# Two modulation vectors computed during the linear attention instead of during the latent attention

## The chip, the cores and the metric

The kernel runs on one core of a Trainium2 chip. The metric is the device time of one execution in microseconds (us); runs of one kernel are summed up by their median. The core has a matrix engine (TensorE, PE in the profile, with its weight loads shown as PEld), three engines for elementwise work (VectorE = DVE, ScalarE = ACT, GpSimd = POOL) and a queue engine (SyncE = SP) that issues most of the transfers between main memory and on-chip memory. Each engine takes its own instructions strictly in the order in which the program gives them, and waits on semaphores for the others.

## The reference, cut to what matters

One layer of a streaming encoder for 1024 prompt tokens and 64 sample tokens. Six vectors of length 1024 per stream (the modulation) are computed from a conditioning vector; the layer uses them at different places.

```python
mod = silu(c) @ w_ada + b_ada                      # w_ada: 1024 x 6144
shift1, scale1, gate1, shift2, scale2, gate2 = split(mod, 6)
h = rms_norm(x, g_norm1) * (1 + scale1) + shift1
proj = h @ w_in
c_q, c_kv, k_rope, gq, gk, gv, g_lr, g_r = split(proj)
a_out = latent_attention(c_q, c_kv, k_rope, ...)   # "latent attention", softmax over keys
b_out = gated_linear_attention(gq, gk, gv, g_lr) * silu(g_r)   # recurrence over chunks of tokens
x = x + gate1 * (concat(a_out, b_out) @ w_out)
h2 = rms_norm(x, g_norm2) * (1 + scale2) + shift2
x = x + gate2 * (square(relu(h2 @ w_up)) @ w_down)
```

The vectors are numbered 0 (shift1), 1 (scale1), 2 (gate1), 3 (shift2), 4 (scale2), 5 (gate2). Vectors 2 to 5 are not needed before the output projection, which comes after both attentions.

## The kernel before, in words

The program writes its work as Python generators ("streams"). `interleave` steps through several of them with a clock of its own: a stream yields how long its last piece keeps PE busy (`pe`), how long it then has to wait (`wait`), and a condition for going on. Of the streams that are ready the first in the list goes next. This gives an order of the program; a scheduler behind it then places each instruction on its engine's queue where its own estimate sees it ready, within the buffers that the program has. The result is one fixed order for each engine.

The stages, with the times of the profile of before:

- 0 to 94 us: the first norm, vectors 1 and 0, and the projection's first two groups of weight columns (A0, A1: queries and keys of the linear attention).
- 94 to about 290 us: the linear attention. The stream `gla` works through nine tiles of tokens (eight of 128, one of 64). For each tile it makes masked scores at seven levels (from halves of 64 tokens down to single ones): DVE and POOL prepare the level's operands `KL` and `QL` (L666 to L675), PE multiplies them (L729), DVE copies the masked result into `ST` (L732). The state `SB` goes on from tile to tile (L746, L755), and L769 and L773 form the tile's output, which ACT and DVE normalise (`og`, L778 and L781) and PE transposes later (L787). Beside it the stream `main` computes the rows of groups B0 and B1 (values, and the gate's low rank input `gl`), in eight steps of three matmuls for each tile of tokens (lines 93 to 95, 128x264), and from the gate rows of a chunk of three tiles the decays `bcum`: transposes L580, a matmul L585, ACT, and the scans L594 on DVE. From about 190 us `main` goes on with the columns of groups C0 and C1, and `latents` with D1.
- to about 388 us: query latents and the keys of the cached frames.
- 388 to about 606 us: the latent attention: keys, queries and three `worker` streams that take score matmuls (L971), softmax, transposes (L1008) and value matmuls (L998). The stream `mods` runs beside them and computes vectors 2, 4, 3, 5 in this order; it needs one of the four PSUM banks named `mm`, which the workers share.
- then the output projection, the second norm and the MLP, to the end.

One modulation vector is `mod_vec(m, ...)`: eight steps over the 1024 rows of `w_ada`. Each step has one 512 KB piece (`raw`, 128x1024) loaded by SP (L155) and four matmuls (L166) whose stationary side is 32 columns wide, one for each 32-column strip of the array, all into one bank. With `ahead=3` the first three pieces are loaded at once, and piece k+3 when step k has been written. After step eight ACT copies the bank (`lat`, L174), PE transposes it in two pieces (L178) and DVE adds the bias (`modT`); vector 4 takes two more small DVE operations (`G12`).

The pieces lie in the pool `rawp`, which has three buffers under one name. The same three buffers hold the raw pieces of `w_in`, which `loader` brings for the next group and which ACT and DVE then split into two halves `wh` and `wl` (L207, L213). `loader` starts group number j once group j-2 has been used up ("end B0" for C0).

```python
        for k in range(KT):
            yield 0, wait, None
            wait = min(wait, after)
            ...
            for j in range(4):
                mm = PE.matmul(acc[32 * j:32 * j + 32, 0:256], lhsT=scT[:, k, :], rhs=was[k][:, 256 * j:256 * (j + 1)],
                               start=(k == 0), stop=(k == KT - 1), tile_position=(0, 32 * j))
            if k + ahead < KT and ahead:
                load(k + ahead)
            yield 500, 0, None
```

## Time and profile before

| | |
|---|---|
| median of 3 runs | 1396.76 us (1396.51 to 1401.75) |
| the profiled execution's own time | 1395.58 us |
| its span, first to last instruction | 1393.8 us, mean granted TensorE clock 0.995 |
| PE busy over the span | 1338.4 us |
| DVE, ACT, POOL busy | 899.3, 654.4, 134.5 us |
| transferred | 188.15 MB, 135 GB/s on average |

The profiled execution's time is 1.8 us longer than its span: what lies before the first and after the last instruction. The profile's views used below are: the page (busy time of each engine, the chain of work that ended last); busy time by stretches, whose columns are the stretch, its length, the busy us and number of records of PE, PEld, DVE, ACT and POOL, then the granted clock (1.00 is full speed), the share of time in which the transfer engines moved data, and GB/s; the timeline of one engine, whose columns are start, length, engine, line, operation and shapes, with a number of records merged in a row and, in brackets, how long the engine stood idle before it and what ended that; and the list of waits. A 4-byte matmul as in L166 or L729 leaves two records.

### The profile page before, as it was taken

Reading aid. Unit: us, or ns where it says so; the run is one execution under the profiler, and the core shown is the slowest. Engines: PE = TensorE matmul, PEld = TensorE weight load, DVE = VectorE, ACT = ScalarE, POOL = GpSimd, SP = SyncE. Lnnn points to the kernel's source line nnn. Section 1 sums busy time; section 2 is a strip of 40 time slices with the busy share of each in tenths; the row PEclk is TensorE's granted clock in tenths of the full one; section 3 lists DMA queues with packets and bytes.
Section 4 is the critical chain, followed back from the end, with each engine's and each line's share of the span. In section 5 each row is a group of like instructions: output and inputs, shape, how many; then the busy total and the mean of one; then the engine's idle time right before and its main releaser. Section 6 shows DMA issues by size and latency. Waiting matters only on the chain.

```text
span 1393.8 us, 26311 instructions
## 1 busy us (share of the span) xinstructions
PE 1338.4 (96%) x10014; PEld 1257.6 (90%) x10014; DVE 899.3 (65%) x2034; ACT 654.4 (47%) x1623; POOL 134.5 (10%) x248
## 2 busy tenths in 40 slices
PE   6999899988999999999998999999999999999998
PEld 5898788887876778899998999999999999999998
DVE  5688777337565766656798756566545866874554
ACT  5465454235345566653475544544444343343342
POOL 0026445111011210000000000000000000000000
PEclk9999999999999999999999999999999999999999
DMA  9320021394253442164225444344348764543440
GB/s 345 121 73 9 16 73 45 114 249 124 86 158 119 152 133 61 52 200 137 78 81 178 159 150 150 128 156 143 102 172 286 281 219 154 184 127 95 125 129 33
DMA packets 165592, 188.15 MB, mean 135 GB/s; under 512 B 16814, under 2 KB 116442, under 8 KB 165466
## 3 DMA queue, kind: packets, MB, share of 16 engines
q1 hardware_dynamic: 158010, 180.90, 40.5%
q10 hardware_dynamic: 7456, 5.57, 1.2%
q8 instruction: 79, 1.29, 0.4%
q14 instruction: 47, 0.39, 0.1%
HBM read 132.97 MB, written 53.46 MB: 134 GB/s over the span
## 4 chain that ended last, share of the span: by engine, by line
PE 80%; DVE 10%; DMA 4%; ACT 3%; POOL 2%; issue 2%; SPq 0%; ACTq 0%; DVEq 0%; POOLq 0%
PE mm L93 14%; PE mm L95 14%; PE mm L94 14%; PE g L93 5%; PE g L95 5%; PE g L94 5%; PE mm L971 3%; PE tp L93 3%; PE tp L95 3%; PE tp L94 3%; PE g L998 3%; PE mm L166 2%; DMA raw<-in_w_in 1%; PE tp L1008 1%; DVE ST L732 1%
## 5 line engine op out<-in xcount | busy, mean ns | idle before, releaser
L101 ACT CAST opers<-quad 128x512 fp32r<-128x512 f32 x112 | 69.5, 620 | 185.0 <-PE mm L95 146.2
L102 DVE TENSOR_TENSOR opers<-quad,opers 128x512 fp32r<-128x512 f32 x112 | 77.3, 690 | 114.0 <-ACT opers L101 114.0
L95 PE MATMUL mm<-opers 128*128 128x272 f32 x448 | 128.9, 288 | 0.0
L93 PE MATMUL mm<-opers 128*128 128x272 f32 x448 | 128.5, 287 | 0.3 <-DVE e L1785 0.3
L94 PE MATMUL mm<-opers 128*128 128x272 f32 x448 | 128.3, 286 | 0.0
L93 PE MATMUL mm<-ah,wh 128*128 128x272 f32 x424 | 122.2, 289 | 4.2 <-ACT wh L101 2.2
L94 PE MATMUL mm<-al,wh 128*128 128x272 f32 x424 | 121.5, 287 | 0.0
L95 PE MATMUL mm<-ah,wl 128*128 128x272 f32 x424 | 121.4, 288 | 0.0
L93 PE MATMUL mm<-hh,wh 128*128 128x384 f32 (+2 forms) x264 | 90.6, 347 | 1.7 <-ACT hh L101 1.7
L95 PE MATMUL mm<-hh,wl 128*128 128x384 f32 (+2 forms) x264 | 87.4, 332 | 0.0
L94 PE MATMUL mm<-hl,wh 128*128 128x384 f32 (+2 forms) x264 | 87.3, 331 | 0.0
L93 PEld LDWEIGHTS mm<-opers 128*128 128x128 f32 x448 | 84.6, 189 | 0.5 <-issue 0.5
L93 PEld LDWEIGHTS mm<-ah,wh 128*128 128x128 f32 x424 | 79.8, 188 | 5.3 <-ACT wh L101 2.6
L95 PEld LDWEIGHTS mm<-opers 128*128 128x128 f32 x448 | 84.3, 188 | 0.0
L94 PEld LDWEIGHTS mm<-opers 128*128 128x128 f32 x448 | 84.0, 188 | 0.0
L94 PEld LDWEIGHTS mm<-al,wh 128*128 128x128 f32 x424 | 79.7, 188 | 0.0
L95 PEld LDWEIGHTS mm<-ah,wl 128*128 128x128 f32 x424 | 79.5, 188 | 0.0
L102 DVE TENSOR_TENSOR opers<-ru,opers 128x544 fp32r<-128x544 f32 x108 | 77.6, 720 | 2.1 <-ACT opers L101 2.0
L101 ACT CAST opers<-ru 128x544 fp32r<-128x544 f32 x108 | 69.4, 643 | 13.1 <-PE mm L95 11.7
L101 ACT CAST wh<-ru 128x512 fp32r<-128x512 f32 x67 | 41.3, 618 | 67.4 <-PE g L94 24.5
L102 DVE TENSOR_TENSOR wl<-ru,wh 128x512 fp32r<-128x512 f32 x67 | 46.0, 690 | 36.4 <-ACT wh L101 36.1
L93 PE MATMUL mm<-wh,hh 128*128 128x264 f32 (+3 forms) x216 | 66.2, 308 | 0.2 <-ACT wh L213 0.2
(409 smaller groups left out, 4338.8 us busy)
## 6 DMA issues: line engine op xcount, KB each, us to landing
ru<-u_d SPq DMA_DIRECT2D x108, 272.0 KB, 2.8
raw<-in_w_ada SPq DMA_DIRECT2D x40, 512.0 KB, 4.0
ru<-in_w_up SPq DMA_DIRECT2D x32, 512.0 KB, 4.1
quad<-in_w_down SPq DMA_DIRECT2D x16, 1024.0 KB, 7.0
u_d<-st SPq DMA_DIRECT2D x60, 272.0 KB, 2.1
u_d<-sc SPq DMA_DIRECT2D x45, 272.0 KB, 2.1
raw<-in_w_in SPq DMA_DIRECT2D x22, 256.0 KB, 4.0
x<-in_xo_T SPq DMA_DIRECT2D x8, 544.0 KB, 5.1
```

What stands on the lines that cost most here:

```text
L93: PE.matmul(out, lhsT=ah, rhs=bh, start=first, stop=False, skip_group_check=more)
L94: PE.matmul(out, lhsT=ah, rhs=bl, start=False, stop=False, skip_group_check=more)
L95: PE.matmul(out, lhsT=al, rhs=bh, start=False, stop=last, skip_group_check=more)
L101: ACT.copy(hi, src)
L102: eng.tensor_tensor(out=lo, in0=src, in1=f32(hi), op=ALU.subtract)
L166: mm = PE.matmul(acc[32 * j:32 * j + 32, 0:256], lhsT=scT[:, k, :], rhs=was[k][:, 256 * j:256 * (j + 1)], start=(k == 0), stop=(k == KT - ...
L732: DVE.copy_predicated(ST[:n, :, :n].rearrange("p c (b r h) -> p c b r h", r=2, h=hf)[:, :, :, 1], masks[:n, mlv, :n // 2].rearrange("p (o ...
L971: PE.matmul(sp[:n, :w], lhsT=x[:, hd, :n], rhs=y[:, hd, :w], start=(j == 0), stop=(j == 4))
L998: PE.matmul(op[:n, 0:P], lhsT=pt[:kw, k, :n], rhs=kvs[kt // 4].v[:kw, kt % 4, hd], start=(kt == 0), stop=(kt == nkt - 1))
L1008: PE.transpose(tp[:kw, k, :n], pr[k0 // 4][:n, P * k:P * k + kw], ident[:n, :n])
```

## The change

Vectors 2 and 4 leave the stream `mods` of the latent attention. A new stream `mods_first` computes them in the linear attention's stage, from the moment at which group B1 is split. It stands in the list behind `gla` and ahead of `main`, so that in `interleave` a step of it goes before rows of B0 and B1 that are ready at the same time. It uses the same three `rawp` buffers, the pool `dp` for the copy of the bank, and one `mm` bank; the step's wait is given as `after=5000`, but `mod_vec` starts at 3500 and takes the smaller of the two, so a step waits 3500 there too. Group C0's loads now wait for "mods 2" as well, since they need the same three buffers.

```diff
@@ loader
             if j >= 2:
-                yield from load_group(key, w_in_cols(a, b), 8, b - a, after=has("end " + GROUPS[j - 2][0]))
+                yield from load_group(key, w_in_cols(a, b), 8, b - a,
+                                      after=has("end " + GROUPS[j - 2][0], *(["mods 2"] if key == "C0" else [])))
@@ linear attention's stage
+        def mods_first():
+
+            yield 0, 2000, has("B1")
+            for m in (2, 4):
+                yield from mod_vec(m, rawp, "raw", dp, mm_bank, 3, after=5000)
+            done.add("mods 2")
+
         lats = Stream(latents())
-        interleave([weights, gla(), main(), gates(), lats], rest=(weights, lats))
+        interleave([weights, gla(), mods_first(), main(), gates(), lats], rest=(weights, lats))
@@ latent attention's stage
     def mods():
-        for m in (2, 4, 3, 5):
+        for m in (3, 5):
```

What this makes of the engines' orders is shown at three places. (Lines from 249 on stand one to eight lower in the changed program: L729 is L730 there, L746 is L747, L773 is L774.)

The first is PE near the end of the linear attention's first tile, in the profile of before from 111.71 to 118.88 us: the tile's state matmul (`kt_`), its last four levels (`QL`, `KL`), the next tile's diagonal (`pr`) and the tile's output (`ST`). Before:

```order
L746 MATMUL g<-gv,kt__1175 128x256 x2
L729 MATMUL g<-QL_904,KL_901 128x128 x2
L729 MATMUL g<-QL_905,KL_902 128x128 x2
L729 MATMUL g<-QL_906,KL_903 128x128 x2
L729 MATMUL g<-QL_904,KL_901 128x128 x2
L705 MATMUL g<-indi,pr 128x2 x2
L773 MATMUL mm<-gv,ST 128x128 x4
```

Now, from the row ahead of the state matmul on:

```order
L166 MATMUL mm<-raw,scT 32x256 x4
L747 MATMUL g<-gv,kt__1185 128x256 x2
L730 MATMUL g<-QL_904,KL_901 128x128 x2
L166 MATMUL mm<-raw,scT 32x256 x3
L730 MATMUL g<-QL_905,KL_902 128x128 x2
L730 MATMUL g<-QL_906,KL_903 128x128 x2
L166 MATMUL mm<-raw,scT 32x256
L730 MATMUL g<-QL_904,KL_901 128x128 x2
L166 MATMUL mm<-raw,scT 32x256 x2
L706 MATMUL g<-indi,pr 128x2 x2
L166 MATMUL mm<-raw,scT 32x256 x5
L774 MATMUL mm<-gv,ST 128x128 x4
```

Between the matmuls of this tile now stand the vector's steps four to eight (their first five matmuls stand a little ahead of these rows, before the tile's third level).

The second is PE where the gates of the second chunk of tiles are made, in the profile of before at 150.98 us: the last `gl` transpose and the gate matmul (`glrT`, `wg`), on whose result the next three tiles' decays rest. Before:

```order
L729 MATMUL g<-QL_905,KL_902 128x128 x2
L769 MATMUL mm<-SB_907,qe 128x256
L580 MATMUL tp<-ident,gl 16x128
L93 MATMUL mm<-wh,hh 128x264
L94 MATMUL mm<-wl,hh 128x264
L95 MATMUL mm<-wh,hl 128x264
L93 MATMUL mm<-wh,hh 128x264
L585 MATMUL g<-glrT_892,wg 128x384 x2
```

Now:

```order
L730 MATMUL g<-QL_906,KL_903 128x128 x2
L166 MATMUL mm<-raw,scT 32x256
L581 MATMUL tp<-ident,gl 16x128
L166 MATMUL mm<-raw,scT 32x256 x3
L770 MATMUL mm<-SB_907,qe 128x256
L586 MATMUL g<-glrT_892,wg 128x384 x2
L774 MATMUL mm<-gv,ST 128x128 x2
L770 MATMUL mm<-SB_907,qe 128x256
L774 MATMUL mm<-gv,ST 128x128 x2
```

The second vector's sixth step stands ahead of the gate matmul, cut in two by the transpose; 14 of the 16 steps stand ahead of it in all. From the fourth tile's state matmul on, PE's order in this stage is that of before again, but for a few exchanges.

The third is SP's queue in the same stage, from the loads of B0 and B1 on. `SB` is the state, `mix_d<-mog` a tile's finished output. Before:

```order
L207 DMA raw<-in_w_in 128x2x264 x8
L207 DMA raw<-in_w_in 128x2x256
L541 DMA wg<-in_b_gate_up 1x256
L207 DMA raw<-in_w_in 128x2x256 x2
L557 DMA SB_909<-in_state_gla 64x128 x4
L791 DMA mix_d<-mog 128x4x128 x4
L207 DMA raw<-in_w_in 128x2x256 x4
```

Now:

```order
L207 DMA raw<-in_w_in 128x2x264 x8
L155 DMA raw<-in_w_ada 128x1024
L542 DMA wg<-in_b_gate_up 1x256
L155 DMA raw<-in_w_ada 128x1024 x2
L558 DMA SB_909<-in_state_gla 64x128 x4
L155 DMA raw<-in_w_ada 128x1024 x9
L792 DMA mix_d<-mog 128x4x128
L155 DMA raw<-in_w_ada 128x1024 x3
L792 DMA mix_d<-mog 128x4x128
L155 DMA raw<-in_w_ada 128x1024
L207 DMA raw<-in_w_in 128x2x256 x3
L792 DMA mix_d<-mog 128x4x128 x2
```

The three early pieces of C0 (128x2x256) have given their places to the vectors' first pieces, and come behind the vectors' sixteenth; the first tile's output stands behind nine loads that wait for PE.

## The prediction

> **What bounds the kernel now.** I read the page first, then the chain of waits, then busy time by stretches of the two stages that the change touches.
>
> ```profile
> PE 1338.4 (96%) x10014; PEld 1257.6 (90%) x10014; DVE 899.3 (65%) x2034; ACT 654.4 (47%) x1623; POOL 134.5 (10%) x248
> PE 80%; DVE 10%; DMA 4%; ACT 3%; POOL 2%; issue 2%; SPq 0%; ACTq 0%; DVEq 0%; POOLq 0%
> ```
>
> PE is the bound of the whole, at 96% busy and 80% of the chain. But the 4% that it lacks lie in few places, so I look at the stretches (stretch, length, then busy us of PE, PEld, DVE, ACT, POOL, granted clock, transfer share, GB/s):
>
> ```profile
> 94.00:124.00 30.00, 25.15 (x158) 22.18 (x157) 22.19 (x71) 16.27 (x57) 17.07 (x34) 0.89 0.07 20
> 124.00:152.00 28.00, 26.71 (x200) 24.51 (x199) 20.55 (x64) 8.80 (x33) 11.77 (x22) 1.00 0.07 20
> 152.00:176.00 24.00, 19.31 (x124) 16.47 (x123) 19.83 (x61) 15.01 (x53) 14.68 (x25) 0.94 0.04 12
> ...
> 196.00:290.00 94.00, 91.14 (x583) 82.56 (x582) 54.83 (x153) 39.59 (x128) 27.36 (x54) 1.00 0.36 108
> ...
> 462.00:535.00 73.00, 71.73 (x532) 57.52 (x532) 48.96 (x142) 44.93 (x145) 10.35 (x14) 1.00 0.44 140
> 535.00:606.00 71.00, 69.65 (x497) 64.64 (x496) 46.77 (x136) 46.37 (x117) 2.66 (x4) 1.00 0.26 76
> ```
>
> The vectors leave a stage in which PE idles 1.27 of 73 and 1.35 of 71 us (462 to 606). They enter one that has idle time: 4.85 us in 94 to 124, 1.29 in 124 to 152, 4.69 in 152 to 176. The transfers are nearly at rest there (share 0.04 to 0.07), so the 8 MB of `w_ada` find room. The question is how much of the idle time lies where the new matmuls are put, and what stands behind them. PE's timeline shows whose waits they are:
>
> ```profile
> 103.86 0.71 PE L729 MATMUL g<-QL,KL 128*128 128x128 f32 x4 [1.39 <-POOL QL L675]
> 110.71 0.68 PE L729 MATMUL g<-QL,KL 128*128 128x128 f32 x4 [1.18 <-DVE sq L591]
> 118.88 2.08 PE L773 MATMUL mm<-gv,ST 128*128 128x128 f32 x8 [0.55 <-DVE dg L707]
> 141.92 0.27 PE L580 MATMUL tp<-ident,gl 128*16 128x128 f32 x1 [1.07 <-DVE gl L578]
> 150.98 1.55 PE L585 MATMUL g<-glrT,wg 33*128 33x384 f32 x4
> 158.90 0.70 PE L769 MATMUL mm<-SB,qe 128*128 128x256 f32 x2 [0.73 <-POOL qe L713]
> 160.01 0.68 PE L729 MATMUL g<-QL,KL 128*128 128x128 f32 x4 [0.41 <-DVE QL L675]
> ```
>
> Around 104 to 119 PE waits for the recurrence's elementwise work, and again from 158. Between, from 124 to 152, it is nearly full: the rows of the second chunk of three tiles have to be made before the gate matmul at 150.98, and DVE and POOL are waiting for that. Whatever is put ahead of the gate matmul in that piece delays it, and everything after it, one for one.
>
> There is a second loss in the stage, the granted clock:
>
> ```profile
> 108.00:110.00 2.00, 1.53 (x7) 0.93 (x6) 0.67 (x3) 1.94 (x6) 0.91 (x2) 1.00 0.00 0
> 110.00:111.00 1.00, 0.29 (x2) 0.32 (x3) 0.83 (x3) 1.00 (x4) 0.00 (x0) 1.00 0.00 0
> 112.00:113.00 1.00, 1.00 (x3) 0.76 (x3) 1.00 (x5) 0.65 (x2) 0.54 (x3) 0.50 0.00 0
> 121.00:122.00 1.00, 1.00 (x6) 1.00 (x6) 0.24 (x1) 1.00 (x8) 0.00 (x0) 0.50 0.00 0
> ```
>
> After a few sparse us (1.53 of 2 and 0.29 of 1 busy) the clock stands at 0.50, and again around 121. Over the 30 us the mean of 0.89 makes 3.3 us of lost clock; the output matmul at 118.88 takes 2.08 us in one of these holes.
>
> **The price of a vector's matmul on PE.** The change moves instructions that the trace shows elsewhere:
>
> ```profile
> 61.15 0.34 PE L94 MATMUL mm<-hl,wh 128*128 128x384 f32 x1
> 61.33 0.34 PE L95 MATMUL mm<-hh,wl 128*128 128x384 f32 x1
> 61.59 0.64 PE L166 MATMUL mm<-raw,scT 128*32 128x256 f32 x8
> 62.16 0.44 PE L93 MATMUL mm<-hh,wh 128*128 128x384 f32 x1
> 62.45 0.34 PE L94 MATMUL mm<-hl,wh 128*128 128x384 f32 x1
> ...
> 43.84 0.62 PE L166 MATMUL mm<-raw,scT 128*32 128x256 f32 x2
> 44.39 0.44 PE L94 MATMUL mm<-hl,wh 128*128 128x384 f32 x1
> ...
> 95.01 0.28 PE L95 MATMUL mm<-wh,hl 128*128 128x264 f32 x1
> 95.13 0.28 PE L93 MATMUL mm<-wh,hh 128*128 128x264 f32 x1
> ...
> 391.25 1.05 PE L166 MATMUL mm<-raw,scT 128*32 128x256 f32 x10
> 392.23 0.83 PE L1207 MATMUL g<-ones,sq 128*128 128x1 f32 x6
> ...
> 466.82 1.50 PE L166 MATMUL mm<-raw,scT 128*32 128x256 f32 x24
> ```
>
> Neighbours follow each other every 0.18 us (61.15 to 61.33). Four vector matmuls in a row (x8 records) run side by side and take 0.57 (61.59 to 62.16). But the step into them is 0.26 and the step out 0.29, where 0.18 each is usual: 0.2 us more. So a run of four costs 0.77. A single one takes 0.55 (43.84 to 44.39), so 0.75 with the same two steps: the price is by run, not by matmul. Five in a row take 0.98 (391.25 to 392.23), twelve 1.5. The Trainium skill (TensorEngine Tiling (Array Packing), Key Properties) says that a change of tiling mode drains the array; these rows agree, with 0.2 us for the two changes. It speaks against this change, which cuts the vectors into more runs: without the 0.2 they would cost 3 us more where they go than where they were, and with it, as counted below, 4.
>
> **What leaves the latent attention.** Up to about 462 us the order there is the old one, with vectors 3 and 5 in the places of 2 and 4. What goes is the second pair of places:
>
> ```profile
> 462.00:535.00 73.00, 10.42 (x128) 2.85 (x128) 1.00 0.44 140
> ...
> L178 PE MATMUL tp<-ident,lat x8: 270/273/293, 425.0 to 533.4; 128*128 128x128 f32 x8
> L174 ACT COPY lat<-mm x4: 372/374/395, 418.0 to 531.9; 128x256 f32<-128x256 f32 x4
> ...
> PE tp L893 <- DVE kn L886: 0.8, 1, 0.8
> ```
>
> The first row is L166 alone: 10.42 us busy for 128 records. By starts it is 9.5: thirteen runs of three or four at 0.57, one of one at 0.55, the run of twelve at 1.5. Fifteen runs at 0.2 add 3.0. The transposes are two pieces of two records for each vector, some 0.45 a vector as starts follow, 0.9 for two. That is 13.4 us off PE. All lie in a stage that is 98% PE; the work that is left has DVE at 49 and ACT at 45 of 73 us, and the `mm` bank that the vectors held until the last copy at 531.9 us is free for the workers. Some gaps that the vectors filled will open: the last row (a wait of PE: total, times, longest) shows one of 0.8 that such a run shortened. I give 1.0 back. If the cover is thinner (each of the fifteen runs was filling a gap of 0.2) it is 3 back. Gain: 12.4, with ends 10.4 and 13.4.
>
> **What enters the linear attention.** Counting runs in the new order: the first vector is cut into eleven (9.1 us: 6.9 by its own starts, among them two of five at 0.98, and 2.2 for the steps), the second into nine (7.4: 5.6 and 1.8). With 0.9 for transposes, 17.4 us come in where 13.4 go. By piece:
>
> 94 to 124: the first vector, 9.1. Its first and third steps stand ahead of gate matmuls, each cut in two, and delay the decays by 1.5 each. The second fills the 1.39 at 103.86; the fourth to eighth, 5.4 us in seven runs, meet the waits from 110 to 119 (1.18, 0.55 and the smaller ones between). Waits in the stretch: 4.85. And PE is then no longer sparse at 108 to 111, so I expect the clock to stay up: 3.3 back at most, since part of the slow clock ran under waits I take 2.0. Sum 9.1 - 4.4 - 2.0 = 2.7. Ends: 0.9 (all waits, all clock) and 7.5 (a third of the waits, no clock).
>
> The Trainium skill (TensorE: Matmul & The Clock Gate, Part 1) has the half clock set in after an idle window of about 3.4 us. Here the longest single wait ahead of it was 1.39 us, so the trace does not agree: a sparse window was enough. By the page's rule the fill could not be what restores the clock, and the sum would be 2.0 worse.
>
> 124 to 152: six steps of the second vector (eight runs, four whole and four cut: 6.1), the last of them on both sides of the `gl` transpose right ahead of the gate matmul, and one vector's transposes, 0.45. Four row matmuls (0.12 each, 95.01 to 95.13) have moved behind it: 0.5 off. The one long wait, 1.07 for `gl`, stays where it is, since the transpose still follows the row directly. Sum 6.1. Ends: 5.0 (the wait filled) and 6.6 (the row matmuls were no loss before).
>
> 152 to 176: steps seven and eight in one run, 1.3, stand just ahead of the wait of 0.73 and the next of 0.41 and fit in; the other transposes meet waits too. 0.
>
> ACT gets two copies (0.37 each, L174), DVE four small operations, both in the recurrence's idle; they stay inside the ends above.
>
> After 176 the order is the old one, and from 196 PE is 97% busy (91.14 of 94), so what PE has lost by then it does not win back: 2.7 + 6.1 + 0 = 8.8 us later.
>
> **Transfers and queues.** Nothing of this waits long by the rows:
>
> ```profile
> raw<-in_w_ada SPq DMA_DIRECT2D x40, 512.0 KB, 4.0
> ...
> 86.44 4.47 SPq L207 DMA_DIRECT2D raw<-in_w_in  x3
> ...
> 191.24 1.56 ACT wh L213 x3
> ```
>
> The first piece is issued about where C0's first was (the last of the three from 86.44 to 90.9) and lands at about 95, when PE comes to it. Later pieces have three buffers and 4.0 us; the tight ones are the seventh and eighth of the first vector, whose buffers, as I estimate from the timeline's starts and the new order, come free at about 113 and 114 and whose matmuls stand at about 117 and 118. C0's pieces are now loaded only after step 16, at about 170, and ACT took the first at 191.24. On SP the first tile's output waits behind nine loads; its buffer is wanted again one tile (some 16 us) later. All this costs 0, and 8 in the rival below.
>
> **Sum.** -12.4 + 8.8 = -3.6 us. The profiled execution (1395.58 us, span 1393.8 and 1.8 around it) becomes 1392.0. It lies 1.2 under the median of the three runs, 1396.76, so for the median I say 1393.2.
>
> **Rivals.**
>
> A, the forecast: 0.50; its own range 1390 to 1398 (12.4 against 0.9 + 5.0 and against 7.5 + 6.1).
>
> B, the waits take nearly all: the chain of the recurrence, not PE, sets the end of the stage. DVE is busy 19.83 of 24 us in 152 to 176, with 4.69 of PE idle there. If DVE starts those tiles better supplied, 3 of PE's 8.8 come back, and the 1.3 of clock that I left out as well: 4.5 later, -7.9 in all, 1389, and 1388 with the upper end of the gain. For it: the waits are real and the order was rearranged around them. Against it: the gate matmul is late for certain, and DVE with it. 0.24.
>
> C, nothing is absorbed: the runs stand a little beside the waits, the clock holes move rather than go, and gaps open in the latent attention: 7.5 + 6.6 against 10.4 is 3.7 later, 1400; with one end only, 1398 to 1399. Then the change is one that only moves PE's work. 0.15.
>
> D, slower: the ring of three buffers. If PE reaches the first vector's seventh and eighth steps before their pieces (4.0 us after their buffers come free), it stands in line, with the levels behind it, and DVE and POOL idle: up to 4.0 each, 8.0 on top of 8.8 is 16.8 against 12.4, 4.4 slower, 1401; with C's gaps up to 1405. It decides from a landing later than 117 us on. Against it: 0.07 transfer share, hence no contention. 0.11.
>
> **How the numbers follow.** Likeliest is A, 1393.2. For 8 in 10 I reach down over B to 1386.5 and up to 1400.5, over C and part of D. About 0.5% (7 us) is what a measurement of this kernel tells from no change: faster by more means under 1389.8, which is most of B and a tenth of A, 0.26; slower by more means over 1403.7, the far ends of C and D, 0.07; between them 0.67.
>
> **What would show it.** The first vector's runs between levels, PE idle in 94 to 124 down from 4.85 to about 1, and the clock near 1.00 there; the second chunk's gate matmul at about 159 to 160 rather than 150.98; the first columns of C0 about 9 us later; from there an unchanged distance to the latent attention; the last vector's transposes (L178) at about 470 instead of 533, and the output projection starting some 4 us earlier than before. I am wrong if the gate matmul moves by under 4 us (B), if a wait of PE for `raw` of over 1 us shows (D), or if the latent attention shortens by under 10 us.

## The result, and the profile after

The changed kernel takes 1401.10 us in the median of 19 executions (1398.89 to 1404.35), the kernel before 1398.39 beside it. The ratio is 1.0018, 95% interval 1.0011 to 1.0025: 2.5 us slower (1.5 to 3.5). That is within the 0.5% that I had called no change, but on the other side of it, and 0.6 us above the range that I gave. The forecast was 3.6 faster. One of the 19 executions of before took 3300.27 us, far outside all the others, and the ratio leaves it out.

The profiled execution takes 1401.34 us (span 1399.5, mean granted clock 0.994), 5.8 more than that of before (1395.58), twice what the medians differ by. So a pair of profiles has to be read with care here; why is shown below.

The page of the changed kernel says as little of it as that of before did: PE 96% busy, 80% of the chain.

```profile
PE 1344.2 (96%) x10014; PEld 1261.4 (90%) x10014; DVE 900.4 (64%) x2034; ACT 654.5 (47%) x1623; POOL 133.1 (10%) x248
PE 80%; DVE 9%; ACT 4%; DMA 3%; POOL 2%; issue 2%; SPq 0%; ACTq 0%; DVEq 0%; POOLq 0%
```

The same stretches as before in the linear attention, of the changed kernel (columns as in the prediction):

```profile
94.00:124.00 30.00, 28.02 (x205) 20.14 (x205) 20.56 (x67) 14.01 (x49) 14.70 (x28) 1.00 0.50 158
124.00:152.00 28.00, 26.78 (x214) 23.01 (x213) 19.15 (x62) 11.20 (x43) 12.83 (x26) 1.00 0.36 114
152.00:176.00 24.00, 22.32 (x167) 17.50 (x167) 17.19 (x55) 12.07 (x41) 9.49 (x18) 1.00 0.23 70
```

In 94 to 124 PE's idle time fell from 4.85 to 1.98 us and the clock went from 0.89 to 1.00. Still the gate matmul of the second chunk is late, and that of the third by as much (timeline of PE, after):

```profile
158.48 0.91 PE L586 MATMUL g<-glrT,wg 33*128 33x384 f32 x2
...
212.04 0.53 PE L586 MATMUL g<-glrT,wg 33*128 33x320 f32 x1
```

Of before the two stood at 150.98 and at

```profile
204.79 0.53 PE L585 MATMUL g<-glrT,wg 33*128 33x320 f32 x1
```

Lateness against before, by the same instruction in both traces:

| instruction | before, us | after, later by |
|---|---|---|
| gate matmul, second chunk | 150.98 | 7.5 |
| gate matmul, third chunk | 204.79 | 7.25 |
| last state matmul (L746) | 260.1 | 7.26 |
| first key transposes (L893) | 323.62 | 8.93 |
| first query transposes of the latent attention (L945) | 404.67 | 8.65 |
| its last output transposes (L1112) | 607.34 | 4.28 |
| last operation of the MLP (L1785) | 1390.23 | 5.67 |

The linear attention costs 7 to 9 us, as predicted. The latent attention gives back 4.4 where 12.4 were predicted. The 1.4 after it come with three stretches of half clock of 3.4 us each (from 727.0, 744.1 and 754.3 us), in code that the change doesn't touch; the profile of before has none there.

Where the gain went shows in the stretch from the old 462.0 to the last output transposes, of before and then of after:

```profile
462.00:607.30 145.30, 142.68 (x1039) 123.46 (x1039) 95.73 (x277) 91.44 (x263) 13.01 (x18) 1.00 0.36 110
```

```profile
470.60:611.60 141.00, 135.07 (x910) 122.59 (x910) 95.82 (x274) 91.27 (x261) 13.34 (x18) 0.99 0.21 61
```

PE is busy 7.6 us less, idle 3.3 more (5.93 against 2.62), and its clock has a hole. The biggest new wait and the hole stand together (timeline of PE, after):

```profile
475.06 0.28 PE L979 MATMUL mm<-kr,qrl 128*128 128x256 f32 x1
477.50 0.33 PE L1016 MATMUL tp<-ident,prob 128*128 128x128 f32 x1 [2.16 <-ACT prob L990]
...
480.69 0.52 PE L94 MATMUL g<-wl,cqh 128*128 128x384 f32 x1
481.01 0.46 PE L95 MATMUL g<-wh,cql 128*128 128x384 f32 x1
481.31 0.34 PE L93 MATMUL g<-wh,cqh 128*128 128x384 f32 x1
481.49 0.34 PE L94 MATMUL g<-wl,cqh 128*128 128x384 f32 x1
```

PE stands 2.16 us until ACT has the probabilities, and then takes 0.32 a matmul (480.69 to 481.01) where 0.18 is usual (481.31 to 481.49): half clock from 477.9 to 481.3, 1.6 us lost over eleven matmuls. In the kernel before the run of twelve vector matmuls (466.82, 1.5 us) stood in this place.

### The profile page after: what moved, and what is told of

Its sections match the earlier page's. It is cut to its first block, busy times and chain, and to the rows that moved or that the text cites. A ratio compares the mean times of both kernels' runs of the same rounds, so it can differ in the third digit from the quotient of the medians.

```text
span 1399.5 us, 26302 instructions
## 1 busy us (share of the span) xinstructions
PE 1344.2 (96%) x10014; PEld 1261.4 (90%) x10014; DVE 900.4 (64%) x2034; ACT 654.5 (47%) x1623; POOL 133.1 (10%) x248
## 4 chain that ended last, share of the span: by engine, by line
PE 80%; DVE 9%; ACT 4%; DMA 3%; POOL 2%; issue 2%; SPq 0%; ACTq 0%; DVEq 0%; POOLq 0%
PE mm L93 15%; PE mm L95 14%; PE mm L94 14%; PE g L93 6%; PE g L95 6%; PE g L94 6%; PE tp L93 3%; PE tp L95 3%; PE tp L94 3%; PE mm L979 2%; PE g L1006 2%; PE mm L166 2%; DMA raw<-in_w_in 1%; PE g L730 1%; PE tp L1016 1%
## 5 line engine op out<-in xcount | busy, mean ns | idle before, releaser
L95 PE MATMUL mm<-opers 128*128 128x272 f32 x448 | 128.9, 288 | 0.0
L94 PE MATMUL mm<-opers 128*128 128x272 f32 x448 | 128.3, 286 | 0.0
L94 PE MATMUL mm<-al,wh 128*128 128x272 f32 x424 | 121.8, 288 | 0.0
L95 PE MATMUL mm<-ah,wl 128*128 128x272 f32 x424 | 121.7, 289 | 0.0
L93 PE MATMUL mm<-hh,wh 128*128 128x384 f32 (+2 forms) x264 | 90.6, 347 | 1.4 <-ACT hh L101 1.4
L95 PE MATMUL mm<-hh,wl 128*128 128x384 f32 (+2 forms) x264 | 87.4, 332 | 0.0
L94 PE MATMUL mm<-hl,wh 128*128 128x384 f32 (+2 forms) x264 | 87.3, 331 | 0.0
L95 PEld LDWEIGHTS mm<-opers 128*128 128x128 f32 x448 | 84.3, 188 | 0.0
L94 PEld LDWEIGHTS mm<-opers 128*128 128x128 f32 x448 | 84.0, 188 | 0.0
L94 PEld LDWEIGHTS mm<-al,wh 128*128 128x128 f32 x424 | 80.0, 189 | 0.0
L95 PEld LDWEIGHTS mm<-ah,wl 128*128 128x128 f32 x424 | 79.9, 189 | 0.0
```

The lines of the kernel that those rows point to most:

```text
L93: PE.matmul(out, lhsT=ah, rhs=bh, start=first, stop=False, skip_group_check=more)
L94: PE.matmul(out, lhsT=ah, rhs=bl, start=False, stop=False, skip_group_check=more)
L95: PE.matmul(out, lhsT=al, rhs=bh, start=False, stop=last, skip_group_check=more)
```

## The experiments

Theories at the outset. **T1**: in the latent attention the vectors' runs filled waits for the softmax, so that taking them out opens the waits; in the linear attention the cost is the steps ahead of the gate matmul. **R1**: the runs were priced too high. **R2**: the new order, not the missing work, costs. **R3**: the linear attention's cost is no matter of the place ahead of the gates, or comes from something else. T2, T3, C1 and C2 came up on the way; the expectations say what they are, and the numbers of the experiments follow their names there.

One thing has to be known to read the numbers. A kernel's executions differ by up to 10 us, and most of that goes with the mean granted clock, which is listed for each. For the kernel before: 1399.8 us in the mean at 0.991 (17 executions), 1398.2 at 0.993 (22), 1396.8 at 0.995 (24). Within the changed kernel and those of the experiments together the slope is 1.0 us for 0.001 of clock (correlation 0.85 over 208 executions); for the kernel before alone it is 0.8 (0.80 over 150). So I split each difference from before into a part of the clock (1.0 us for each 0.001 that the mean clock is lower) and the rest, which is work and waits. The split is my own reckoning, good to some 0.5 us, and to 1 us where the clock's part is large. The first column is the ratio of the runs with its interval, turned into us:

| run | against before, us (95%) | of the clock | rest |
|---|---|---|---|
| the change | +2.5 (1.5 to 3.5) | -2.2 | +4.9 |
| E1 latent attention's part alone | -5.3 (-7.1 to -3.5) | +0.7 | -6.0 |
| E2 linear attention's part alone | +7.7 (5.7 to 9.6) | -2.9 | +10.1 |
| E7 as E1, old order | -4.1 (-6.2 to -2.0) | +0.8 | -4.3 |
| E8 empty steps in the linear attention | +0.3 (-1.3 to 1.8) | +0.2 | 0.0 |
| E9 the change, old order | +3.8 (2.1 to 5.5) | -1.3 | +4.8 |
| E3 the change, later places | +5.3 (3.8 to 7.0) | +1.1 | +4.2 |
| E12 as E1, second places kept | -1.0 (-2.5 to 0.6) | +4.3 | -5.3 |
| E10 the change, second places kept | +6.2 (3.9 to 8.2) | +0.6 | +6.0 |
| F1 E12 with matmuls of no use, misplaced | +1.3 (-0.7 to 3.2) | +4.2 | -3.4 |
| F4 E12 with such in the wait | -1.3 (-2.9 to 0.4) | +3.0 | -4.8 |
| F2 before with such | +1.7 (0.0 to 3.5) | -1.2 | +3.3 |
| F3 the change with such | +3.8 (2.2 to 5.3) | -1.0 | +5.0 |
| F5 the change, one transpose moved | +3.2 (1.4 to 5.0) | -1.4 | +4.8 |
| F6 E1, one transpose moved | -4.1 (-5.7 to -2.2) | +0.8 | -5.4 |
| E5 second vector later | +2.7 (1.3 to 4.1) | -1.7 | +4.4 |
| E4 one vector only | -1.4 (-3.1 to 0.1) | -3.4 | +1.7 |
| E11 as E4, three later places | +0.6 (-0.8 to 2.1) | -1.2 | +2.1 |
| G1 as E4, behind the rows | -4.6 (-6.2 to -3.1) | -2.8 | -1.5 |

(The two parts are of the difference of the means, so they don't always add up to the first column. For the change, the mean and the clock of before are those of the 150 executions beside the later runs.)

### E1 and E2: the two halves

E1 leaves vectors 2 and 4 out; E2 computes them twice.

```diff
-        for m in (2, 4, 3, 5):          # E1, from before
+        for m in (3, 5):
```
```diff
-        for m in (3, 5):                # E2, from the change
+        for m in (2, 4, 3, 5):
```

> The kernel before with vectors 3 and 5 alone in the latent attention; vectors 2 and 4 are left out altogether (ones stand in their place). So only what the change takes out of the latent attention is seen, none of what it puts into the linear attention. Price of the prediction: 12.4 us shorter than before. T1 (the vectors' runs were filler there: PE has less to do, but then waits for the softmax and loses some clock): 4 to 6 us shorter, with new PE waits on probabilities in the stretch where vectors 3 and 5 no longer follow 2 and 4. R1 (the runs were simply priced too high, no new waits): 7 to 9 us shorter, with PE's idle time in the latent attention unchanged at about 2.6 us.

> The changed kernel, but with all four vectors computed in the latent attention as before, so that vectors 2 and 4 are computed twice: the linear attention's part of the change alone. T1: 7 to 9 us slower than before, with the second chunk's gate matmul about 7.3 us later as in the changed kernel, and the latent attention as long as before. The prediction's 8.8 is in this too. R3 (part of the change's loss comes from the two places acting together, such as clock or bank order): under 5 us.

E1 gained 5.3, E2 lost 7.7; they add up to the change (2.4 against 2.5), in the clock (-2.2) and in the rest (+4.1 against +4.9) as well. E1 has the very waits of the changed kernel:

```profile
468.59 0.33 PE L1010 MATMUL tp<-ident,prob 128*128 128x128 f32 x1 [2.16 <-ACT prob L984]
```

and, in its stretch, the same busy time as the changed kernel:

```profile
462.00:603.00 141.00, 134.77 (x908) 122.29 (x907) 95.57 (x273) 91.04 (x260) 13.35 (x18) 0.99 0.21 61
```

T1's numbers fit both; R1's 7 to 9 with idle time unchanged doesn't (6.23 us idle of 141.00, against 2.62 of 145.30 before), and the interplay of R3 is out. In E2's profile the latent attention is as long as before (0.1 longer). The error of the prediction's sum lies in the latent attention alone.

### E7, E8, E9: is it the order?

The scheduler's order also changed around the vectors' places. In E7 and E9 the plan counts the absent steps there as if they were made; in E8 the linear attention has the new plan with empty steps.

```diff
+    def no_vec(after=3500):             # the yields of mod_vec, and no instruction
...
+        for m in (2, 4):                # E7 and E9: behind vectors 3 and 5
+            yield 500, 0, lambda: state["banks"] < 4 and has("UQ")()
+            state["banks"] += 1
+            yield from no_vec()
+            state["banks"] -= 1
```
```diff
-                yield from mod_vec(m, rawp, "raw", dp, mm_bank, 3, after=5000)   # E8
+                yield from no_vec(after=5000)
```

> As the first experiment, vectors 2 and 4 left out (ones in their place), but the plan still counts their steps where the second pair of vectors stood in the latent attention, without issuing anything for them; so the other work there stays almost in the order of before, and the vectors' places are simply empty. The first experiment gained 5.3. T1 (the runs filled waits; with less work on PE the waits open whatever the order): 4 to 6 us shorter than before, PE idle in the latent attention 5 to 6 us. R2 (the new order, not the missing filler, cost the gain): 8 to 11 us shorter, with PE idle near the 2.6 of before.

> The changed kernel with all four vectors in the latent attention as before, and in the linear attention only the plan's steps for two vectors, which issue nothing: so the linear attention has the order that the change gives it and C0's weights are loaded as late, without the vectors' matmuls, loads and copies. T2 (the vectors' own PE work is what costs 7 to 8.6 us there): 1 us either way of before, with the dips of the clock from 108 to 124 us and at 172 back. R2 (the rearranged order or the later load of C0 costs): 2 to 5 us slower than before.

> The changed kernel, whole, with the plan in the latent attention counting the second pair's steps as in the seventh experiment, so that the other work there keeps almost its old order. T1: as the changed kernel, 2 to 3 us slower than before. R2: 1 to 4 us faster than before.

4.1 gained, nothing lost, 3.8 lost. In the latent attention R2 falls with E7 and E9: PE's order there is that of before but for some 70 of 1182 instructions, and E7 gained no more than E1, which has the changed kernel's order there to the instruction. E8 says less than its expectation has it. Without the vectors' work the scheduler gave another order than the changed kernel's (against that some 150 of 1029 instructions of PE stand elsewhere between 90 and 267 us, against before some 90), and its trace has C0's first three loads at 90.6 to 95.1 us as in before, not at 158.0 to 165.9 as in the changed kernel. So E8 shows that the plan's empty steps cost nothing. T2 (the vectors' own work is what costs in the linear attention) fits it, but no run has the changed kernel's order or its later load of C0 without that work. In the changed kernel's trace PE has no wait for `wh` of over 0.15 us between 190 and 300 us, so the later load shows no cost there.

Since E7 nearly keeps the order, its trace can be laid beside that of before, run by run. One place where a run is gone and nothing opened, of before and (from the second row on) of E7, whose first row is the wait that did open:

```profile
505.81 0.34 PE L95 MATMUL g<-wh,cql 128*128 128x384 f32 x1
506.08 0.64 PE L166 MATMUL mm<-raw,scT 128*32 128x256 f32 x8
506.65 0.44 PE L93 MATMUL g<-wh,cqh 128*128 128x384 f32 x1
506.92 0.34 PE L94 MATMUL g<-wl,cqh 128*128 128x384 f32 x1
```

```profile
470.97 0.48 PE L1020 MATMUL tp<-ident,prob 128*128 128x128 f32 x1 [2.17 <-ACT prob L994]
...
507.27 0.34 PE L95 MATMUL g<-wh,cql 128*128 128x384 f32 x1
507.44 0.34 PE L93 MATMUL g<-wh,cqh 128*128 128x384 f32 x1
507.62 0.34 PE L94 MATMUL g<-wl,cqh 128*128 128x384 f32 x1
```

From L95 to L94 it is 1.11 us there and 0.35 here: the run was worth 0.76, my price (0.77). So R1 falls too. What failed is how many runs were worth their price. Laid side by side, of the twelve runs from 475 us on nine bring the rest forward by 0.65 to 1.0 each; the one at 491.81 brings 0.4, and those at 499.58 and 514.11 bring nothing, where E7 now waits. Between 463 and 474 us, where a run of four, the run of twelve and a single one have gone (0.77, 1.7 and 0.75 by the prices), it comes 1.9 us later: there the wait of 2.17 opens, and half clock follows it. E7's latent attention is 4.0 shorter than before's, 9.4 less than the price of 13.4; that place alone makes 5.1 of it, and the three runs that brought little or nothing some 2. In its stretch PE idles 6.7 us (2.62 before), as T1 had it and not R2.

### E3, E12, E10, E11: other places in the latent attention

If the runs are cover, perhaps only some need to stay. E3 spreads vectors 3 and 5 (pace 8500 instead of 3500). E12 and E10 put them into the second pair of places, with empty steps ahead; E11 does so for E4, below.

```diff
+        for _ in range(2):              # E12 and E10; E11 with range(1)
+            yield 500, 0, lambda: state["banks"] < 4 and has("UQ")()
+            state["banks"] += 1
+            yield from no_vec()
+            state["banks"] -= 1
         for m in (3, 5):
```

> The changed kernel, with the steps of vectors 3 and 5 spread over more of the latent attention (8500 in place of 3500 between two steps), so that runs of vector matmuls again stand between its rows to the end of the stretch they filled before. The same work, elsewhere. T1 (the runs are filler for waits on the softmax): 2 to 4 us faster than the changed kernel, so about 0 against before, and PE's idle time in the latent attention back from 5.9 us to about 3. R1 (prices only): as the changed kernel, 2 to 3 us slower than before.

> Vectors 2 and 4 are left out (ones in their place) as in the kernel with the latent attention's part alone, but vectors 3 and 5 now stand in the second pair of places, where vectors 3 and 5 stood before, and the first pair of places is empty: the plan counts those steps and issues nothing. The kernel with the second places empty gained 4.1 to 5.3 us; there one wait of 2.17 us of PE for the probabilities and a half clock behind it opened at about 470 us, where a run of six steps had stood. T3 (that one place gave the gain back; elsewhere a removed run is worth its 0.6 to 0.7 us): 8 to 11 us shorter than before, no PE wait of over 1.3 us in the latent attention and its clock at 1.00. T1 (the runs covered waits everywhere): 4 to 6 us shorter, with new waits in the first places.

> The changed kernel, whole, with vectors 3 and 5 in the second pair of places of the latent attention in the same way. T3: 7.7 to 8.6 lost in the linear attention, 8 to 11 gained in the latent attention: 0 to 3 us faster than before. T1: 2 to 4 us slower, as the changed kernel.

> Half of the change (vector 2 alone in the linear attention), with the first of the four places in the latent attention empty and vectors 4, 3 and 5 in the other three. The half measured 1.4 us faster than before with the last place empty. T3: 4.5 lost in the linear attention, 4 to 6 gained in the latent attention: 0 to 2 us faster. T1: 1 to 2 us slower, the attention's gain being 2 to 3 then.

E3 was to bear out T1 and went against it: it was 2.8 us slower than the change (in its profile PE's largest wait for probabilities is now 2.94 us, at 595). So a run is not a cover of fixed worth that can be put anywhere in the stage. E12 gained 1.0, less than E1, so T3 (it is one place) falls: emptying the first places opens other holes. (The run at about 470 us in that expectation is twelve matmuls, three steps and not six.) E10 lost 6.2, more than T1 or T3 had said, and E11 can't be told from before. E12's profile has half clock for 13.7 us:

```profile
436.00:456.00 20.00, 18.29 (x78) 14.66 (x77) 9.17 (x34) 9.42 (x34) 1.16 (x3) 0.66 0.03 7
```

0.34 of 20 us is 6.8 us. By the split E12's rest is -5.3, much like E1's -6.0; the clock takes 4.3 of it back.

### F1, F4, F2, F3: matmuls of no use in the waits

C1: the waits bring the half clock on, and it takes the gain back. C2: it doesn't hang on them. `fill(bank, k)` puts k matmuls of the identity by itself into a bank that the next instruction overwrites. F1 and F4 add it to E12, F2 to the linear attention's first tile of before, F3 to the change.

```diff
+    def fill(out, k):
+        for _ in range(k):
+            PE.matmul(out[:, 0:P], lhsT=ident, rhs=ident, start=True, stop=True)
...
+            if (i, hd, k0) == (8, 3, 0):    # F1; F4: (8, 2, 0), 4; F3: (1, 0, 0), 16
+                fill(bank, 9)
```

> As the kernel with vectors 2 and 4 left out and vectors 3 and 5 in the second pair of places (1.0 us shorter than before), with nine 128x128 matmuls of the identity by itself, which compute nothing that is used, just ahead of the transposes of the probabilities for which PE waited 1.24 us at 439.35 us, ahead of a clock of 0.50 from 439 to 452 us. C1 (the half clock sets in because PE stood idle there, and it is the half clock that takes the gain back): the clock stays at 1.00 from 436 to 456 us, and the kernel is 6 to 8 us shorter than before. C2 (the half clock comes from elsewhere, or PE would have waited for the others at full clock anyway): within 1 us of the kernel without the nine, 0 to 2 us shorter than before.

> The kernel before, whole, with matmuls of no use in the waits of the linear attention's first tile (ten ahead of the first level's scores, nine ahead of the third's, two each ahead of the fifth's and seventh's, three and four ahead of the next small products), about 0.11 us each, fewer than each wait holds. C1: the clock of 0.50 at 112 to 115 and at 119 to 122 us is gone, and the kernel is 1 to 3 us faster than before. C2: the clock dips as before, or it stays up and the chain of the recurrence takes the time instead: within 1 us of before.

> The changed kernel, whole, with sixteen such matmuls ahead of the transposes of the probabilities for which PE waits 2.16 us at 477.5 us in the changed kernel. With them the order also puts the 18 matmuls of the query projection, which need nothing late, ahead of those transposes instead of behind them. C1: the wait and the clock of 0.50 behind it (2.2 and 1.6 us) go, the sixteen cost 1.8: 1 to 3 us faster than the changed kernel, so within 1.5 us of before. C2: as the changed kernel or up to 2 us slower, 2 to 5 us slower than before.

> Vectors 2 and 4 left out and vectors 3 and 5 in the second pair of places (1.0 us shorter than before), with four matmuls of no use, 0.23 us each, ahead of the transposes for which PE waited 1.24 us at 439.35 us. C1 (the wait brings on the half clock, and the half clock takes the gain back): the clock stays at 1.00 from 436 to 456 us, and the kernel is 6 to 8 us shorter than before. C2: the half clock sets in all the same, 0 to 2 us shorter than before.

One such matmul takes 0.23 us, twice what I had priced, and in F1 they stood at another head, 8 us too early: F1 only shows that the wait and the hole stay when the work is put elsewhere, and costs its nine times 0.23. F4 hit the wait (0.74 left of 1.24), and its profiled execution is what C1 expected, 1388.07 us with the clock whole in that stretch:

```profile
434.00:454.00 20.00, 17.60 (x106) 13.90 (x107) 12.12 (x41) 12.10 (x45) 2.87 (x4) 1.00 0.07 18
```

But the median of its twelve is 1396.77, and their mean clock 0.9904 (E12: 0.9892; before 0.9934). One execution had the luck that most of the eleven others had not. So C1 as I put it falls: filling one wait makes a hole rarer at best. F2 lost 1.7, its fill being dearer than I had priced it; its clock rose by 1.2 us' worth, and its profile still has half clock from 111.2 us. F3's sixteen, 3.7 us of work where PE had waited 2.2, can't be told from the change (+3.8 against +2.5, the intervals overlap).

That the clock is partly chance shows best where nothing differs. E8 has the latent attention of before, instruction for instruction, 2.5 us later. Before, then E8:

```profile
436.00:456.00 20.00, 18.65 (x126) 12.78 (x124) 11.20 (x39) 10.28 (x42) 2.84 (x4) 1.00 0.39 122
```

```profile
438.00:458.00 20.00, 18.82 (x122) 13.00 (x121) 9.81 (x35) 10.08 (x39) 1.34 (x2) 0.91 0.38 112
```

The same wait for probabilities (1.06 us in both) is followed by half clock in one execution and not in the other.

### F5 and F6: one transpose moved

In the changed kernel a transpose of probabilities stands ahead of 18 matmuls of the query projection. Holding it to the order of the program moves this one row behind the 18, and nothing else on PE.

```diff
+                mv = PE.transpose(tp[:kw, k, :n], ...)
+                if (i, hd) == (1, 0):
+                    tc.keep_in_program_order(mv)
```

> The changed kernel, whole, with one transpose of probabilities moved on PE, from ahead of the query projection's 18 matmuls to behind them (the row of one joins the row of five). If the wait of 2.16 us and the half clock behind it (1.6 us) are what that place costs: 3 to 4 us faster than the changed kernel, so 0 to 2 us faster than before, with the clock at 1.00 from 476 to 484 us. If what PE saves there is waited for again at the next probabilities: within 1 us of the changed kernel, 1.5 to 3.5 us slower than before.

> Vectors 2 and 4 left out, as in the kernel with the latent attention's part alone, with the same transpose moved behind the same 18 matmuls. The former gained 5.3. If that place is what took the gain back: 8 to 10 us shorter than before. If not: 4.5 to 6.5 us shorter.

Nothing came of it (+3.2 and -4.1; +2.5 and -5.3 without). The trace of F5 says why, and shows that my expectation for F3 was wrong in "need nothing late":

```profile
473.86 0.28 PE L979 MATMUL mm<-kr,qrl 128*128 128x256 f32 x1
476.07 0.45 PE L93 MATMUL g<-wh,cqh 128*128 128x384 f32 x1 [1.93 <-DVE v L888]
```

The 18 write into a `g` bank that DVE has yet to empty (its copy of `v`). At this place both things that PE could do next wait for DVE or ACT, in either order; the vectors' run that stood here had waited for neither. That is T1, at its plainest.

### E5, E4, G1: the linear attention

E5 starts the second vector after the fourth tile's gate. E4 makes half of the change: vector 2 in the linear attention, 4, 3 and 5 in the latent. G1 is E4 with the vector's stream behind the row stream in the list.

```diff
+                if m == 4:                  # E5
+                    yield 0, 0, has("gates 3")
```
```diff
-            for m in (2, 4):                # E4 and G1
+            for m in (2,):
...
-        for m in (3, 5):
+        for m in (4, 3, 5):
```
```diff
-        interleave([weights, gla(), mods_first(), main(), gates(), lats], rest=(weights, lats))   # G1
+        interleave([weights, gla(), main(), mods_first(), gates(), lats], rest=(weights, lats))
```

> The changed kernel, with vector 4 started only after the fourth gate of the linear attention's chunks is through, so that of its steps only two matmuls' worth stands ahead of the second chunk's gate matmul. T1 (PE sets the pace ahead of that gate matmul, and each step there costs its full price, while later ones meet waits for DVE): the gate matmul 1.5 to 3 us later than before instead of 7.5, and the whole 1 to 3 us faster than before. R3 (the cost comes wherever in the linear attention the steps stand): the whole 2 to 3 us slower than before, as the changed kernel.

> Half of the change: vector 2 alone in the linear attention, vectors 4, 3 and 5 in the latent attention. T2 (each vector's work is paid at much the same price wherever it stands in the linear attention): half of the changed kernel's loss, about 1 us slower than before (4 lost in the linear attention, 2 to 3 won in the latent attention). R3 (the first vector fits into waits and slow clock, the second pays): 0 to 3 us faster than before, with the second chunk's gate matmul under 3 us later than before.

> Half of the change (vector 2 alone in the linear attention), with its steps placed behind the row matmuls in the plan: none stands ahead of the first tiles' gate matmuls, and 20 of its 32 matmuls stand in seven runs between the levels of the first tile, where the kernel before has its waits. The half as measured was 1.4 us faster than before, at the edge of what can be told. If the steps ahead of the gate matmuls were what the vector cost, and the clock stays up: 2 to 4 us faster than before, the second chunk's gate matmul under 3 us later than before. If the cost is the vector's work wherever it stands in the linear attention: 0 to 2 us faster, as the half was, and the gate matmul 4 to 5 us later.

In E5 the second chunk's gate matmul came 3.7 later instead of 7.5, but the third's 7.1 later, and the whole lost as much as the change: T1's point on the linear attention falls for the second vector. By these traces the stage has room for about one.

E4 was at the edge of a gain. Of its gate matmuls, that of the first chunk's last tiles (107.97 us in before) and that of the second chunk (150.98):

```profile
111.08 1.13 PE L586 MATMUL g<-glrT,wg 33*128 33x256 f32 x4
...
154.28 1.55 PE L586 MATMUL g<-glrT,wg 33*128 33x384 f32 x4
```

Three of the vector's eight steps stand ahead of the first of these, which is 3.1 later than before. At the second, behind all eight steps, it is 3.3: the last five cost next to nothing, since the waits and the two stretches of half clock that before's profile has there (from 111.9 and 118.7) make room for them. (The third chunk's gate is 4.7 later, but E4's profile has half clock from 198.2 to 201.6 us, between the two.) G1 has none of the steps ahead of the first, and its gates stand at

```profile
108.08 1.13 PE L586 MATMUL g<-glrT,wg 33*128 33x256 f32 x4
...
150.12 1.55 PE L586 MATMUL g<-glrT,wg 33*128 33x384 f32 x4
```

The second is 0.9 earlier than before. The third stands at 206.26, 1.5 later, with half clock from 178.5 to 181.9 us between. G1 is a clear gain, 0.9967 (0.9956 to 0.9978). Stretches of G1:

```profile
94.00:124.00 30.00, 28.10 (x214) 22.86 (x213) 23.00 (x75) 17.02 (x59) 17.43 (x34) 1.00 0.40 132
...
110.99 0.71 PE L730 MATMUL g<-QL,KL 128*128 128x128 f32 x4
```

The last row, from its timeline, is the level that waited 1.18 at 110.71 before. Nine vector matmuls now stand in that wait, and it starts 0.28 later. The latent attention, with three vectors left as cover, still shortens by 2.8 in this profile (1.7 late at L945's first, 1.0 early at L1112's last), and the mean clock of G1's executions is 0.9961 (0.9934 for before beside them). So for the first vector T1 holds: what it cost was its three steps ahead of the first chunk's gate matmuls.

## Why the prediction was wrong, point by point

**The term that failed is "-12.4, latent attention".** Measured alone (E1) it is -5.3. Its price of work, 13.4, held where it could be read by itself (0.76 for a run, against 0.77). What failed is "I give 1.0 back", with 3 at worst, for the waits that the runs had covered. Of the 13.4 the changed kernel kept 4.3 in that stretch. 3.3 came back as idle time that the trace shows and 1.6 as half clock; the other 4.2 are what subtraction leaves. E7, which fell short by about as much, shows where: 5.1 at one place and some 2 at three other runs that brought little or nothing. F5's profile, whose latent attention has no half clock, bears the clock's part out: it is 6.2 shorter than before's, the changed kernel's 4.4. I had read "98% PE" as PE setting the pace, with DVE at 49 and ACT at 45 of 73 us as proof of slack. But PE was at 98% with the vectors in it, and their runs waited for none of the softmax's steps. Without them it has 135.07 of 141 us, and at the place of the longest run the chain scores, maximum, exponential, transposes sets the pace (the wait of 2.16 for the probabilities, and F5). Counting one wait of 0.8 as what a run had covered looked at the waits that were left, not at those that the runs had closed.

**"+8.8, linear attention" held as a sum.** 7.5 and 7.3 at the gates, 8.7 at the latent attention's start, 7.7 in E2. Its parts held less well. At the second chunk's gate one vector is 3.3 late (E4), where I had 2.7 for 94 to 124; the second adds 4.2 (7.5 less 3.3), where I had 6.1 for 124 to 152, less than the lower end of 5.0. For the first vector I saw that two of its steps delay the decays "by 1.5 each"; that delay is nearly all that it costs, and what came behind it went into waits and clock, as I had it.

**"-2.0, the clock"** there was right in kind: 2.9 by the split in E2, and the profile of before has three stretches of half clock between 94 and 290 us (from 111.9, 118.7 and 173.3), that of the changed kernel none. What I left out is that the clock pays in the other stage as well. The Trainium skill (TensorE: Matmul & The Clock Gate, Part 1) has a free-running window of about 3.4 us, after an idle one of which the clock halves. The length agrees with these traces: but for the program's end, half clock comes in whole stretches of 3.41 us, one (477.9 to 481.3 here) to four on end (E12), on one grid that runs through an execution. That the window must be idle does not agree. Cut along that grid, the twenty traces have 80 stretches at full clock with PE busy for less than half of them (by the profile's modelled busy time), and 69 of these are followed by half clock; with PE busy for 0.50 to 0.85 it is 36 of 574, and above that none of 7303. Of the changed kernel, the stretch with the wait of 2.16 us and the one behind it:

```profile
474.44:477.86 3.42, 1.26 (x11) 1.06 (x10) 3.24 (x13) 2.69 (x13) 1.33 (x2) 1.00 0.00 0
477.86:481.27 3.41, 3.41 (x12) 3.41 (x11) 2.26 (x9) 1.21 (x7) 0.00 (x0) 0.50 0.00 0
```

The place of the grid alone doesn't explain why the same code is hit in one execution and spared in another: in before and in E8 the wait of 1.06 us ends 2.2 and 2.0 us into its stretch, and PE is busy for 0.69 of both stretches.

**The rivals.** B is out: the gate matmul moved by 7.5. D is out: the longest wait of PE for `raw` in these profiles is 0.63 us, in E5. So its number, 1401, was met by luck. C (1398 to 1400) is right for the latent attention ("gaps open"), wrong for the linear one, where waits and clock were absorbed. The sign that I had named came true: the latent attention shortened by less than 10.

**The signs.** The clock at 1.00 in 94 to 124, the vectors' last transposes at 473.2 (I said 470), the gate matmul at 158.5 (159 to 160): all seen, or nearly. The first columns of C0 came 7.2 later (about 9). PE idle in 94 to 124 was 1.98, where I said about 1. The output projection 4 earlier: 3.9 later instead.

Still open is why the clock halves after one wait and not after a like one, which these runs show but don't settle; and the 1.4 us lost between the last state matmul and the latent attention, which range from 2.8 lost (E10) to 1.2 won (F5, the one trace without half clock between 290 and 405 us).

## What to carry to other kernels

Before you price work that leaves a stage at 98% of its engine, ask which of its instructions wait for nobody: those are the cover, and taking them out gains only what does not wait behind them. Take the order of before without them and look where two dependent steps now meet; leaving the work out altogether (E1) is the cheapest test of the gain. Work that is put into waits pays if it stands behind what other engines wait for: of the same vector 3.3 us late at the second chunk's gate became 0.9 early by changing places with the rows, and half of the change so placed is 4.6 us faster than the kernel before.

## What the runs showed of the hardware

The mean granted clock varies between executions of one kernel (0.988 to 0.998 over the 150 of the kernel before), and most of the spread in time goes with it: 1.0 us for 0.001. Half clock comes in whole stretches of 3.41 us, and 69 of 80 such stretches in which PE was busy for less than half were followed by one, none of 7303 with PE busy for over 0.85. A single profile can so be 8.7 us from its kernel's median (F4: 1388.07 against 1396.77). Sparse stretches lower the mean: 0.9892 with the first places empty, 0.9959 with a vector in the waits of the linear attention, 0.9931 before.
